# Second layer of a two-layer decoder: the first pair's triangular solution in two parts, and two receptance mixes with priority

## The chip, the cores and the metric

The kernel runs on one core of one Trainium2 chip. A core has a matrix engine (PE, with its weight loads shown apart as PEld), a vector engine (DVE), a scalar engine (ACT), GpSimd (POOL) and a queue engine (SP) that only issues transfers; each works through its own instructions in order, and they meet through semaphores. The metric is the device time of one execution, in microseconds. A time is given as the median of several runs.

## The reference, cut to what matters

Two residual layers on x of 512 rows by 2048 columns, in float32. Layer 0 is differential attention and is not touched. Layer 1 is RWKV-7 time mixing with 32 heads of 64:

```python
p = h @ w_in
p = p + (token_shift(p) - p) * mu                 # mix of each row with the row before it
r, k, v, g, dw, da = jnp.split(p, RW_SPLITS, axis=-1)
w_log = -softplus(-(w0 + tanh(dw) @ decay_up)) - 0.5
decay = jnp.exp(-jnp.exp(w_log))
a = sigmoid(a0 + da @ iclr_up)
kk = heads(k * k_k); kk = kk / max(norm(kk), 1e-12)
k = k * (1.0 + (a - 1.0) * k_a)
# per row t:  sa = S @ (-kk_t)
#             S  = S * decay_t + sa (kk_t * a_t)^T + v_t k_t^T
#             y_t = S @ r_t
y = group_norm(y) + sum(r * k * r_k) * v
x = x + (y * silu(g)) @ w_out
```

The scan over rows is computed in 8 chunks of 64 rows. Within a chunk the recurrence of `sa` becomes a triangular system, which is solved once per chunk and head, so that the chunks then need only matrix products.

## The kernel before, in words

Every product with a weight matrix is done in three passes (`mm3`, L122): operands are split into a high and a low half, and the three products high·high, low·high, high·low add up in one PSUM bank. Weights arrive by transfer in `wraw`; ACT makes the high half `wh` (L105) and DVE the low half `wl` (L106), 8 blocks of 128 by 128 at a time.

**Rounds.** Layer 1 works on 16 pairs of heads (128 channels), j = 0 to 15, in one loop of `layer1`. A projection of one pair (`proj`, through `unit_chan`) is 48 products in a row. Round j has, in the order of the program:

- from j = 1 on, the start of the scan of pair j-1 (`chain(...).step`), whose later steps are put between the products of the round, a fixed number of products apart (`tick`);
- `stage2(j)`: DVE scales the receptance of pair j into `p.AR` (L1291) and makes the product `rf` from it (L1292);
- the projection of the values, `proj(2, j)`. Behind its 18th product comes `behind`: `gram` (PE products `pt` L1301 and `gp` L1318, which read `p.AR` and `p.BK`), the copies of `gp` to SBUF, their transfer to DRAM (`ltd`, SP), the masks on POOL (L1339, L1341) and `t_solve`;
- `stage_v` (mix of the values L1144/L1145, and `y`, L1448, which reads a bank of tag `pd`), in round 1 the first gate's projection, then `begin(j + 1)` (projection and mix of the keys of the next pair, and its decays), in rounds 3 and later a gate, then `receptances(j + 1)`: the projection and its mix (`shift_mix`, ACT L1144 and then DVE L1145).

**The solution.** `t_solve(j)` loads `LT` back from DRAM in another layout and makes 31 steps on DVE. Step i is two instructions, L1377 (`tmpl<-LT,Tm`) and L1379 (`Tm<-Tm,tmpl`); it works on (31-i) columns by (i//4 + 1) rows, which is how a step is recognised by its size in the trace (step 19 is 12·5 = 60 elements a partition). Each step needs the step before. Then L1386 scales the result and SP writes it to DRAM (`td<-Tm`, L1387). For pairs 3 to 14 the steps come in three parts (`PARTS` = 0, 21, 29, 31), of which the second and third are held until steps of the scan have been issued. For pairs 0, 1, 2 and 15 all 31 steps are issued at once.

**What follows it.** `t_combine` reads `td` back into `TT` by four transfers on SP (L1406), and DVE transposes (L1416) give `T1`. PE then makes the small products `px` (L1422, in the bank of tag `pd`; later L1433), and then the scan of the 8 chunks (`sm`, L1510, L1521, L1528) begins. For pair 0 the transposes come 64 products after the start of round 1 (`leads = {1: 64, ...}`) and `px` 8 products later (`GAP_T`).

**The order.** A planner orders the instructions of each engine. It plays the program through with its own estimates of durations and, each time an engine is free, picks the ready instruction with the lowest number. The number is the place in the program, less the offset of `high_priority`: 2000 for `urgent` functions (`split_w`, `shift_mix`), 3000 (`SCAN`) for steps of a chain, 4000 (`SOLVE`) for the solution, 8000 (2·`SOLVE`) for `p.AR` of pairs 1 and 2. Offsets of nested blocks add up. `issue_after(x)` puts what its block holds behind x on x's engine. On the chip each engine keeps the planned order, whether or not the estimates were right.

## Time and profile before

| what | us |
|---|---|
| median of 3 runs (lowest to highest) | 2072.66 (2071.66 to 2075.58) |
| profiled execution, its own time | 2070.32 |
| span of its instructions | 2068.6 |
| PE busy | 2051.0 |
| PEld busy | 1680.1 |
| DVE busy | 1605.3 |
| ACT busy | 1122.7 |
| POOL busy | 383.2 |

The span runs from the first to the last instruction of the program; the execution's own time has a little around it. Layer 1's rounds begin about 940 us into the span and the rounds 0 to 2, of which the change speaks, lie between 940 and 1130 us. Products on PE overlap: one is shown with 0.39 us, but the next begins 0.23 us after it, so that in the rows it is the starts and the idle times that count.

In a timeline row the first number is the start in us from the start of the span, the second the duration in us, then engine, line, operation, output<-inputs and shapes; a bracket at the end is the time for which the engine sat idle before, and what released it. In a row of the chain of waits the first number is the start and the second what it takes on the chain.

### The profile page before, as it was taken

The page shows a single profiled execution, that of the slowest core. Times are in us where ns is not written, and L with a number is a line of the kernel's source. Part 1 is how long each engine was busy: PE and PEld are TensorE (multiplying, and loading weights), DVE is VectorE, ACT ScalarE, POOL GpSimd, SP SyncE. Part 2 cuts the span into 40 slices and gives each one's busy share as a digit, 9 for nine tenths or more (in the row PEclk, how much of TensorE's full clock was granted, in tenths as well). Part 3 has the DMA queues.
Part 4 walks back from the last instruction along what each step waited for, and adds up shares of the span by engine and source line. Part 5 has one row for each costly group of instructions (what it writes and reads, how often), then busy time and mean ns, then how long its engine had stood idle before and what let it go on. Part 6 is the DMA issues. An engine that isn't in the chain of part 4 may idle for free.

```text
span 2068.6 us, 34162 instructions
## 1 busy us (share of the span) xinstructions
PE 2051.0 (99%) x11948; PEld 1680.1 (81%) x11948; DVE 1605.3 (78%) x4113; ACT 1122.7 (54%) x2238; POOL 383.2 (19%) x765
## 2 busy tenths in 40 slices
PE   9999999999999999999999999999999999999999
PEld 7888888888888888878777778888888888877887
DVE  6988988888888976475778887877777878777645
ACT  5765656555666544355555555555555555545322
POOL 1021211102011100101122322222222222232001
PEclk9999999999999999999999999999999999999999
DMA  8487978778787965723323223233333232346565
GB/s 273 140 177 195 172 177 183 166 195 162 189 179 169 263 223 174 170 86 108 102 82 98 86 85 97 79 104 98 97 97 97 86 96 81 112 127 203 184 164 121
DMA packets 158653, 294.61 MB, mean 142 GB/s; under 512 B 64416, under 2 KB 81824, under 8 KB 158480
## 3 DMA queue, kind: packets, MB, share of 16 engines
q1 hardware_dynamic: 110912, 184.91, 28.6%
q0 software_dynamic: 24928, 87.21, 22.4%
q10 hardware_dynamic: 22640, 20.30, 3.0%
q8 instruction: 94, 1.54, 0.3%
q14 instruction: 79, 0.65, 0.1%
HBM read 268.71 MB, written 23.66 MB: 141 GB/s over the span
## 4 chain that ended last, share of the span: by engine, by line
PE 86%; DVE 9%; ACT 2%; DMA 1%; issue 1%; ACTq 0%; SPq 0%; DVEq 0%; POOLq 0%
PE pp L122 43%; PE pp L573 22%; PE pt L122 5%; DVE wl L106 2%; PE sm L1510 2%; PE gp L1318 1%; PE sc L122 1%; PE o L122 1%; PE sm L1528 1%; PE sm L1521 1%; PE lora L122 1%; PE z L122 1%; DVE tmpl L1377 1%; DMA pair<-in_xT_dram 1%; PE Y L1550 1%
## 5 line engine op out<-in xcount | busy, mean ns | idle before, releaser
L106 DVE TENSOR_TENSOR wl<-wraw,wh 128x1024 fp32r<-128x1024 f32 (+2 forms) x291 | 356.6, 1225 | 189.6 <-ACT wh L105 179.3
L105 ACT CAST wh<-wraw 128x1024 fp32r<-128x1024 f32 (+2 forms) x291 | 303.6, 1043 | 271.7 <-PE pp L122 135.3
L122 PE MATMUL pp<-hL,wh 128*128 128x512 f32 x1024 | 414.6, 405 | 0.0
L122 PE MATMUL pp<-hH,wl 128*128 128x512 f32 x1024 | 413.5, 404 | 0.0
L122 PE MATMUL pp<-hH,wh 128*128 128x512 f32 x1024 | 413.2, 403 | 0.0
L122 PEld LDWEIGHTS pp<-hH,wh 128*128 128x128 f32 x1024 | 193.3, 189 | 34.5 <-issue 0.4
L122 PEld LDWEIGHTS pp<-hL,wh 128*128 128x128 f32 x1024 | 193.3, 189 | 33.6
L122 PEld LDWEIGHTS pp<-hH,wl 128*128 128x128 f32 x1024 | 193.5, 189 | 32.3
L573 PE MATMUL pp<-wh,hH 128*128 128x512 f32 x448 | 177.0, 395 | 0.0
L573 PE MATMUL pp<-wh,hL 128*128 128x512 f32 x448 | 176.0, 393 | 0.0
L122 PE MATMUL pp<-wh,hH 128*128 128x512 f32 x372 | 146.8, 395 | 1.7 <-ACT hH L1104 1.7
L122 PE MATMUL pp<-wh,hL 128*128 128x512 f32 x372 | 147.0, 395 | 0.1
L122 PE MATMUL pp<-wl,hH 128*128 128x512 f32 x372 | 146.5, 394 | 0.5 <-DVE wl L106 0.5
L1377 DVE SCALAR_TENSOR_TENSOR tmpl<-LT,Tm 128x60 f32<-128x60 f32 (+24 forms) x496 | 134.4, 271 | 13.3
L573 PE MATMUL pp<-wl,hH 128*128 128x512 f32 x448 | 140.4, 392 | 0.0
L1516 POOL COPY SA<-VS 64x64 f32<-64x64 f32 x224 | 56.7, 253 | 416.7 <-DVE VS L1532 381.9
L1379 DVE TENSOR_TENSOR Tm<-Tm,tmpl 128x60 f32<-128x60 f32 (+24 forms) x496 | 104.2, 210 | 11.7
L1513 ACT COPY rhs<-sm 64x64 f32<-64x64 f32 x256 | 52.8, 206 | 91.8 <-PE sm L1510 89.2
L573 PEld LDWEIGHTS pp<-wl,hH 128*128 128x128 f32 x448 | 84.5, 189 | 17.1
L573 PEld LDWEIGHTS pp<-wh,hH 128*128 128x128 f32 x448 | 84.2, 188 | 17.3 <-issue 0.3
L573 PEld LDWEIGHTS pp<-wh,hL 128*128 128x128 f32 x448 | 84.3, 188 | 16.2
L1523 ACT COPY VS<-sm 64x64 f32<-64x64 f32 x256 | 52.7, 206 | 72.6 <-PE sm L1521 66.0
(402 smaller groups left out, 4380.7 us busy)
## 6 DMA issues: line engine op xcount, KB each, us to landing
wraw<-in_rw_w_in_dram SPq DMA_DIRECT2D x128, 512.0 KB
wraw<-in_da_w_in_dram SPq DMA_DIRECT2D x75, 512.0 KB
wraw<-in_da_w_in_dram POOLq DMA_DIRECT2D x28, 512.0 KB, 6.5
wraw<-in_da_w_out_dram SPq DMA_DIRECT2D x26, 512.0 KB
wraw<-in_rw_w_out_dram SPq DMA_DIRECT2D x26, 512.0 KB
Ta<-in_da_w_in_dram POOLq DMA_DIRECT2D x21, 512.0 KB, 5.4
Tb<-in_da_w_in_dram POOLq DMA_DIRECT2D x21, 512.0 KB, 5.4
Tc<-in_da_w_in_dram POOLq DMA_DIRECT2D x21, 512.0 KB, 5.4
```

The source lines that it names most:

```text
L105: a = nc.scalar.copy(hi[:, ks], raw[:, ks])
L106: d = nc.vector.tensor_sub(lo[:, ks], raw[:, ks], hi[:, ks].bitcast(F32))
L122: m = nc.tensor.matmul(out, a, b, start=s, stop=e, skip_group_check=skip)
L573: m = nc.tensor.matmul(out[t][:], x, wt[lo][:, k, :], start=first, stop=end and lo == 1 and k == KG - 1, skip_group_check=True)
L1318: m = nc.tensor.matmul(gp[h][:, i * P : (i + 1) * P], BK[r_, c0 + i, :, :], p.AR[r_, c0 + i, :, :], start=True, stop=True)
L1377: nc.vector.scalar_tensor_tensor(tt, LT[:, i : i + 1, i + 1 :].to_broadcast([P, s, n]), n2[:, i : i + 1], Tm[:, 0:s, i : i + 1].to_broadca ...
L1379: nc.vector.tensor_add(Tm[:, 0:s, i + 1 :], Tm[:, 0:s, i + 1 :], tt)
L1510: nc.tensor.matmul(sm[:, 0:P], both(p.G[:, c, 0]), both(VS[:, c]), start=True, stop=True)
L1513: nc.scalar.copy(rhs[r_, :], sm[r_, h * C : h * C + C])
L1516: nc.gpsimd.tensor_copy(p.SA[r_, c - 1, :], VS[r_, c, h, :])
L1521: nc.tensor.matmul(sm[:, P : P + C], both(g.TT[j % 2][:, c]), rhs[:], start=True, stop=True)
L1523: g.copied = nc.scalar.copy(VS[r_, c, h, :], sm[r_, P : P + C])
```

## The change

Three things are altered, all in layer 1.

1. The solution of pair 0 is made in two parts, steps 0 to 18 and steps 19 to 30. The first is issued where all of it was issued before. The second is issued at the head of round 1, right after `stage2(1)`, with an offset of 4000 (no longer 8000, since it is no longer inside `t_solve`) and, on DVE, behind the instruction that scales the receptance of pair 1 (L1291). The final scaling and the transfer `td<-Tm` go with the second part.
2. In round 1 `stage2` stands before the start of the scan of pair 0, in place of after it.
3. The mixes of the receptances of pairs 1 and 2 get an offset of 8000 on top of the 2000 that `shift_mix` has. Their projections keep theirs.

`t_solve` now takes the list of parts: (0, 19, 31) for pair 0, `PARTS` for pairs 3 to 14 as before, (0, 31) for pairs 1, 2 and 15, which is one part, issued at once as before.

```diff
     with g.tc.high_priority(offset=2 * SOLVE if 0 < j <= LAG else 0):
-        nc.vector.tensor_mul(p.AR[:, :, 1, :], ..., p.E[:, :, 1:])
+        scaled = nc.vector.tensor_mul(p.AR[:, :, 1, :], ..., p.E[:, :, 1:])
...
+    return scaled
...
     def parts():
-        for a, b in zip(PARTS, PARTS[1:]):
-            with g.tc.high_priority(offset=SOLVE), g.tc.issue_after(g.state.ins) if a and split else ExitStack():
+        for a, b in zip(split, split[1:]):
+            with g.tc.high_priority(offset=SOLVE), g.tc.issue_after(g.state.ins) if a else ExitStack():
                 steps(a, b)
...
-            if split:
-                yield
+            yield
...
         def receptances(j):
-            return shift_mix(g, proj(0, j), P, *mus(g, 0, j), "r", 1)
+            ps = proj(0, j)
+            with tc.high_priority(offset=2 * SOLVE if 0 < j <= LAG else 0):
+                return shift_mix(g, ps, P, *mus(g, 0, j), "r", 1)
...
+            if j == 1:
+                g.state = stage2(g, j, r, p)
+                next(pairs[0].solve)
+                g.state = None
             if j:
                 others = ...
                 chain(g, j - 1, pairs[j - 1], 5, *gaps, others, leads.get(j, GAP_D - GAP_T)).step(g)
-            stage2(g, j, r, p)
+            if j != 1:
+                stage2(g, j, r, p)
...
-                loaded = t_solve(g, j, p, LAG < j < D // P - 1)
+                loaded = t_solve(g, j, p, (0, 19, HALF - 1) if j == 0 else PARTS if LAG < j < D // P - 1 else (0, HALF - 1))
```

More of the change, by code (lines that the diff above doesn't have):

```diff
@@ L1290, in stage2 @@
     with g.tc.high_priority(offset=2 * SOLVE if 0 < j <= LAG else 0):
-        nc.vector.tensor_mul(p.AR[:, :, 1, :], r[:].rearrange("p (c t) -> p c t", c=NC_), p.E[:, :, 1:])
+        scaled = nc.vector.tensor_mul(p.AR[:, :, 1, :], r[:].rearrange("p (c t) -> p c t", c=NC_), p.E[:, :, 1:])
     nc.vector.scalar_tensor_tensor(r[:], r[:], col("hrk"), p.f[:], ALU.mult, ALU.mult)
     p.rf = r
+    return scaled
 def gram(g, j, p, before):
```

## The prediction

> **What bounds the kernel now.** First the page's busy times, then the waits of PE in rounds 0 to 4 of layer 1 (930 to 1240 us), then stretches of 20 us.

> ```profile
> span 2068.6 us, 34162 instructions
> PE 2051.0 (99%) x11948; PEld 1680.1 (81%) x11948; DVE 1605.3 (78%) x4113; ACT 1122.7 (54%) x2238; POOL 383.2 (19%) x765
> ```
> ```profile
> PE sm L1510 <- DVE VS L1532: 2.6, 7, 0.9
> PE gp L1318 <- DVE AR L1291: 0.9, 1, 0.9
> PE pt L1459 <- DVE y L1448: 0.2, 1, 0.2
> PE px L1422 <- DVE y L1448: 0.2, 1, 0.2
> ```
> ```profile
> 980.00:1000.00 20.00, 20.00 (x89) 16.49 (x89) 18.70 (x54) 10.44 (x17) 0.00 (x0) 1.00 0.23 80
> 1000.00:1020.00 20.00, 18.94 (x142) 15.16 (x141) 14.22 (x32) 8.09 (x14) 5.44 (x13) 1.00 0.46 128
> 1240.00:1299.00 59.00, 59.00 (x439) 48.91 (x434) 46.72 (x130) 32.72 (x77) 16.27 (x38) 1.00 0.32 94
> ```

> The columns of a stretch are its length, then PE, PEld, DVE, ACT and POOL busy, and the granted clock. PE is busy for all of 980 to 1000 and of 1240 to 1299, at full clock: the later rounds have nothing to give. In the whole span PE is idle for 2068.6 - 2051.0 = 17.6 us, and the change adds or removes no PE instruction. From 1000 to 1020, where the second pair's receptance is scaled and the first pair's solution ends, PE is idle 20.00 - 18.94 = 1.06 us, which is the 0.87 of `gp` and the 0.19 of `px` below. That is about all that the edits of round 1 can win at their own places.

> The trace's LDWEIGHTS says something else at first sight. [...] By it PE has 19% to spare (81% on the page), and what 1000 to 1020 loses against the full stretch before it is 16.49 - 15.16 = 1.33 us in place of 1.06: the ceiling of the gain would be 1.33. The trace bears that out only in part: the full stretch has itself 16.49 of 20.00, 82%, without any idle time, so 81% is near to what this kernel's products allow.

> Now the place itself, in the rows of the engines in order of time.

> ```profile
> 996.90 1.06 ACT L105 CAST wh<-wraw 128x1024 fp32r<-128x1024 f32 x1 [3.10 <-PE pp L122]
> 997.86 0.68 ACT L1144 ACTIVATE mixr<-pp,omu 128x512 f32<-128x512 f32 x1
> ```
> ```profile
> 997.94 0.28 DVE L1377 SCALAR_TENSOR_TENSOR tmpl<-LT,Tm 128x60 f32<-128x60 f32 x1
> 998.25 0.22 DVE L1379 TENSOR_TENSOR Tm<-Tm,tmpl 128x60 f32<-128x60 f32 x1
> ...
> 999.55 1.22 DVE L106 TENSOR_TENSOR wl<-wraw,wh 128x1024 fp32r<-128x1024 f32 x1
> 1000.68 0.27 DVE L1377 SCALAR_TENSOR_TENSOR tmpl<-LT,Tm 128x54 f32<-128x54 f32 x1
> 1000.87 0.74 DVE L1145 SCALAR_TENSOR_TENSOR mixr<-pp,mu,mixr 128x511 f32<-128x511 f32 x1
> 1001.53 0.21 DVE L1379 TENSOR_TENSOR Tm<-Tm,tmpl 128x54 f32<-128x54 f32 x1
> 1001.65 0.69 DVE L1291 TENSOR_TENSOR AR<-mixr,E 128x512 f32<-128x512 f32 x1
> ```
> ```profile
> 1001.10 0.42 PE L1301 MATMUL pt<-k,ones 128*32 128x128 f32 x8
> 1002.40 2.06 PE L1318 MATMUL gp<-AR,BK 64*128 64x128 f32 x32 [0.87 <-DVE AR L1291]
> ...
> 1006.33 0.39 PE L122 MATMUL pp<-hH,wl 128*128 128x512 f32 x1
> ```

> The receptance's mix is ready for DVE when ACT ends its share, at 997.86 + 0.68 = 998.54, but DVE comes to it at 1000.87, after steps 19 to 21 of the solution (the first of them at 997.94) and a `wl`. `AR` follows at 1001.65, and PE, in order, stands 0.87 before `gp`. What comes after on the chain of waits is the solution:

> ```profile
> 1008.95 0.43 DVE Tm L1386
> 1009.43 2.17 DMA td<-Tm
> 1011.69 3.56 DMA TT<-td
> 1015.27 0.44 DVE T L1416
> 1015.71 0.63 DVE mixv L1145
> 1016.37 0.45 DVE T L1416
> 1016.85 0.70 DVE y L1448
> ...
> 1017.59 0.69 PE px L1422 x32
> ```

> So the next thing for which PE stands, 15 us later, hangs on the end of the solution, and with only 0.19 us of idle PE (the `px` row of the waits) the two are all but tied. That is the centre of the forecast.

> **The parts of the change.**

> *Mix with priority, and steps 19 to 30 behind `AR`.* Steps 19, 20, 21 and the first half of 22 no longer stand ahead of `AR`. DVE reaches the end of step 18 at 997.9. With the `wl` first (its ACT half ends at 996.90 + 1.06 = 997.96) it is 998.0 + 1.2 = 999.2, then the mix 0.7 and `AR` 0.7: 1000.6. With the mix first it is 998.54 + 0.7 + 0.7 = 999.9. PE could take `gp` some 0.4 after `pt` starts at 1001.10, so at 1001.5: both orders are early. The wait of 0.87 goes: -0.87, and PE is 0.87 ahead from `gp` on.

> *The end of the solution.* From 997.9 to 1009.4 DVE stands still only for hand-overs, and the same instructions have to be done before the final scaling in both kernels. Moving steps behind `AR` changes their order and not their sum. What is added is the idle time in which DVE has no more step it may do and the mix is not ready: nothing if the `wl` fills it (997.96 against 997.9, so 0.05), and 998.54 - 997.91 = 0.63 if the mix is planned ahead of the `wl`. I take 0.05: on ACT the `wl`'s half is planned ahead of the mix's, so it is the `wl` that is there first. An offset of 4000 in place of 8000 costs nothing, since the weights' 2000 and the scan's 3000 stay behind it. It could end earlier by what is let in between two steps now and later then: at most the `wl`, 1.2.

> *What is late next.* PE now comes to `px` at 1017.59 - 0.19 - 0.87 = 1016.53, and the transposes and `y` (which holds the bank of `px`) are done at 1016.85 + 0.70 + 0.05. So PE stands until 1017.59 + 0.05, 1.11 us in place of 0.19. What `gp` gave, `px` takes: -0.87 + 0.92 = +0.05.

> *`stage2` ahead of the scan's start in round 1.* The scan's start issues four transfers on SP (`TT`) that wait for `td` anyhow, at 1011.69, ten us after `AR`; on DVE and PE it issues nothing before `px`'s transposes. It moves past no work that is ready: 0.

> *The transfers that go with the second part.* One `td<-Tm` (1009.43 on the chain), still followed by `TT`. What stands behind it on SP:

> ```profile
> 1009.92 1.05 SPq L1330 DMA_DIRECT2D ltd<-G  x2
> 1011.02 0.44 SPq L78 DMA_DIRECT2D wraw<-in_rw_w_in_dram  x1
> 1011.69 2.81 SPq L1406 DMA_DIRECT2D TT<-td  x4
> 1014.54 0.45 SPq L1330 DMA_DIRECT2D ltd<-G  x1
> 1015.09 6.03 SPq L78 DMA_DIRECT2D wraw<-in_rw_w_in_dram  x2
> ```

> `gp` comes 0.87 earlier, so its copies and `ltd<-G` do too; they stand behind `td` or `TT` now and lose nothing. 0.

> *Round 2's mix.* The chain of waits shows `pt` and `gp` of round 2 back to back:

> ```profile
> 1063.72 0.36 PE pt L1301 x8
> 1064.07 1.99 PE gp L1318 x32
> ```

> There is no wait to remove; an earlier mix shifts other DVE work by its 0.7 us, and the only DVE work for which PE stands in that stretch is the scan's `VS` (2.6 us over seven places in 300 us). 0, between -0.4 and +0.7.

> The sum is +0.05 us on a profiled execution of 2070.32 with a span of 2068.6. That execution lies 2.34 below the median of the runs, 2072.66, and a difference carries over: 2072.7.

> **Rivals.**

> *The gain is kept.* DVE takes the values' mix and `y` ahead of the two transposes, which stand idle for `TT` until 1015.27. Then the transposes end at 1015.27 + 0.9 = 1016.2, before PE is there (1016.53), and both waits are gone: -1.06, 2071.6. For it: the planner holds the solution's end for later than before, and the values' mix then comes first. Against: nothing on the chip changes by more than tenths.

> *The `wl` starves.* If it is planned behind the whole second part it ends near 1009.4, where the first product that reads it comes at 1006.33 - 0.87 = 1005.46. PE stands 3.9, less the 0.87 and the 0.19: +2.9, 2075.6. Against: before, it slipped in between two steps, and the chain of steps leaves such holes still.

> *Slower: `TT` falls behind a weight load on SP.* The place is SP at 1015.09, where a load stands that goes when its buffer comes free. If the planner holds the solution's end for so late that this load is put ahead of `TT`, the four transfers begin at 1015.5 and not at 1011.69, and `px`, which is tied to them, moves by all of it: +3.8, with the idle 0.63 +4.4, 2077.1. It decides from the moment that the planner's estimate of the end moves by 1015.09 - 1011.69 = 3.4 us. Against: the second part has about four steps more behind `AR` than before (19 to 22), at 0.53 us each (997.94 to 998.47 above), some 2 us.

> *Not what it says.* The wait of `gp` stays, if the DVE reaches `AR` late all the same: 0, 2072.7; the same time as the forecast.

> **How the numbers follow.** The wait moves to `px`: 0.55. Gain kept: 0.25. `wl` late: 0.06. `TT` behind a load: 0.06. No effect: 0.08. A measurement of this kernel can tell about 0.2%, 4.1 us, from no change; of the cases only the `TT` one passes it. Runs of the same kernel spread from 1.0 below to 2.9 above the median, so I give each side a little for that: faster 0.04, same 0.88, slower 0.08. The range reaches from the kept gain in a low run, 2072.66 - 1.06 - 1.0 = 2070.6, to the late `wl`, 2075.6, and by a quarter of the scan's 2.6 us of waits (0.6) further at both ends, since round 1's order on DVE may shift for or against `VS`: 2070.0 to 2076.2.

> **What would show it.** Right: no row of PE `gp` waiting for `AR`; on DVE `AR` at 999.9 to 1000.6 with twelve steps behind it (the first of 60 elements); `td<-Tm` at 1009.4 to 1010.1; PE at `px` waiting about 1.1 for `y` or the transposes; the rounds from 1240 on shifted as a whole by tenths. Kept gain: `mixv` and `y` ahead of both L1416. Wrong: `td<-Tm` after 1011, a wait of a `pp` product for `wl`, or rounds from 1240 on that are not 59 us apart.

## The result, and the profile after

The changed kernel takes 2076.11 us (median of 22 runs, 2072.93 to 2078.64), the kernel before 2070.30 (22 runs, 2069.19 to 2075.58). The ratio is 1.0024, with a 95% interval of 1.0018 to 1.0029: slower by some 5 us (5.8 between the medians), a little more than the 0.2% that the prediction took as the least that can be told. The forecast was 2072.7, with 0.88 on no difference that can be told. The time came out just inside the upper end of its range, 2076.2, and that is luck: the range stood on the 2072.66 of three runs, while 22 runs put the kernel before at 2070.30. The same terms on that base end at 2073.8. How the loss comes about is not what the prediction said. The profiled execution took 2076.41, 6.1 more than the one of before (2070.32).

First the page's busy times, then the two largest waits of PE in 930 to 1240 us (total, times, longest), both of the changed kernel:

```profile
span 2074.7 us, 34161 instructions
PE 2053.3 (99%) x11948; PEld 1680.3 (81%) x11948; DVE 1606.4 (77%) x4113; ACT 1124.2 (54%) x2238; POOL 381.4 (18%) x765
```
```profile
PE px L1422 <- DVE T L1416: 3.9, 2, 3.2
PE sm L1510 <- DVE VS L1532: 2.0, 5, 0.9
```

The row of `gp` is gone, as the change intends. In its place stands `px`, with 3.9 us where it had 0.2. Matmuls are as many as before; PE's busy time grew by 2.3 us all the same; some 1.7 of it is the clock (3.41 us at half, below).

PE's order is the same in both kernels, so the same product can be looked up in both traces. How far the changed kernel is behind at some of them:

| product | before | after | behind | added since the row above |
|---|---|---|---|---|
| `pt`, ahead of all that changed | 975.48 | 976.18 | 0.70 | 0.70 |
| `gp` of round 1 | 1002.40 | 1002.15 | -0.25 | -0.95 |
| `px` of round 1, its third | 1017.64 | 1021.37 | 3.73 | 3.98 |
| sixth product behind `px` | 1019.48 | 1024.65 | 5.17 | 1.44 |
| `sm` of the seventh chunk of the first pair's scan | 1050.63 | 1055.20 | 4.57 | -0.60 |
| `gp` of round 6 | 1296.75 | 1303.21 | 6.46 | 1.89 |
| end of the span | 2068.6 | 2074.7 | 6.1 | -0.4 |

The first 0.70 is a difference between two executions. In round 6 PE stood 1.6 for `AR`; the run split_only below, whose planned order is the same, shows no such wait, so it too belongs to the execution. What is left is round 1: -0.95 + 3.98 + 1.44 = 4.5 us.

Round 1 on DVE, in order of time (start, duration, instruction):

```profile
998.36 0.23 DVE L1380 TENSOR_TENSOR Tm<-Tm,tmpl 128x65 f32<-128x65 f32 x1
998.68 1.23 DVE L106 TENSOR_TENSOR wl<-wraw,wh 128x1024 fp32r<-128x1024 f32 x1
999.83 0.74 DVE L1145 SCALAR_TENSOR_TENSOR mixr<-pp,mu,mixr 128x511 f32<-128x511 f32 x1
1000.60 0.69 DVE L1291 TENSOR_TENSOR AR<-mixr,E 128x512 f32<-128x512 f32 x1
1001.21 0.28 DVE L1378 SCALAR_TENSOR_TENSOR tmpl<-LT,Tm 128x60 f32<-128x60 f32 x1
...
1009.56 0.23 DVE L1378 SCALAR_TENSOR_TENSOR tmpl<-LT,Tm 128x8 f32<-128x8 f32 x1
1009.71 1.22 DVE L106 TENSOR_TENSOR wl<-wraw,wh 128x1024 fp32r<-128x1024 f32 x1
1010.85 0.17 DVE L1380 TENSOR_TENSOR Tm<-Tm,tmpl 128x8 f32<-128x8 f32 x1
1011.05 0.42 DVE L1387 TENSOR_TENSOR Tm<-Tm,LT 128x256 f32<-128x256 f32 x1
...
1013.35 0.74 DVE L1145 SCALAR_TENSOR_TENSOR mixv<-pp,mu,mixv 128x511 f32<-128x511 f32 x1
1014.20 0.69 DVE L1448 TENSOR_TENSOR y<-pt,mixv 128x512 f32<-128x512 f32 x1
1019.88 0.44 DVE L1416 STREAM_TRANSPOSE T<-TT 64x256 f32<-64x256 f32 x1 [4.99 <-DMA TT<-td]
```

`AR` follows step 18, one `wl` and the mix, and twelve steps follow it. But a second `wl` (1009.71) has slipped between the two halves of the last step. From the end of step 18 (998.59) to the end of the scaling (1011.47) it is 12.88 us; before, it was 1009.37 - 997.91 = 11.46. So the solution is 1.42 late, 1.22 of it that `wl`. After it DVE has `mixv` and `y` done by 1014.9, and then stands 4.99 us for a transfer.

The queues tell why. SP (changed kernel), then POOL's load of the second pair's `LT`, changed kernel and kernel before:

```profile
1004.93 1.81 SPq L1331 DMA_DIRECT2D ltd<-G  x4
1010.96 0.35 SPq L78 DMA_DIRECT2D wraw<-in_rw_w_in_dram  x1
1011.54 0.39 SPq L1388 DMA_DIRECT2D td<-Tm  x1
1018.01 1.81 SPq L1406 DMA_DIRECT2D TT<-td  x4
```
```profile
1011.77 2.00 POOL L1365 DMA_DIRECT2D LT<-ltd  x4 [4.53 <-DVE Tm L1387]
```
```profile
1016.97 2.00 POOL L1364 DMA_DIRECT2D LT<-ltd  x4 [4.31 <-DMA ltd<-G]
```

Before, only one of the second pair's four `ltd<-G` stood ahead of `td<-Tm` on SP, two and a weight load behind it, and the fourth behind `TT` (1014.54). POOL's `LT` loads, which need all four and the buffer that the end of the solution gives free, could not start before 1016.97. Now all four `ltd<-G` and the weight load of 1010.96 are planned ahead of `td`. The weight load is issued 0.6 us before `td`. The last thing for which the `LT` loads wait is now the solution itself (the releaser in the row is `Tm`, no longer `ltd`), so they start 0.2 us behind `td`. The solution's transfers run beside both. The chain of waits of the changed kernel:

```profile
1011.05 0.44 DVE Tm L1387
...
1011.54 6.34 DMA td<-Tm
...
1018.88 1.97 DMA TT<-td
1020.88 0.45 DVE T L1416
...
1021.37 1.05 PE px L1422 x30
```

`td` took 6.34 in place of 2.17 us. The 1.97 of `TT` is not to be set against the 3.56 of before: it runs from the third of the four transfers, the 3.56 from the first (on SP the four begin at 1018.01). From the end of the scaling to the start of the last transpose it is 1020.88 - 1011.47 = 9.4 us in place of 1016.37 - 1009.37 = 7.0.

What PE does in that time, changed kernel, and the stretches (length; PE, PEld, DVE, ACT, POOL busy; granted clock; DMA share; GB/s):

```profile
1016.81 0.39 PE L122 MATMUL pp<-hH,wl 128*128 128x512 f32 x1
1020.37 0.24 PE L1422 MATMUL px<-T,G 32*32 32x32 f32 x2 [3.17 <-DVE T L1416]
1021.37 1.05 PE L1422 MATMUL px<-T,G 32*32 32x32 f32 x30 [0.76 <-DVE T L1416]
...
1022.95 0.63 PE L122 MATMUL pp<-hL,wh 128*128 128x512 f32 x1
1023.37 0.63 PE L122 MATMUL pp<-hH,wl 128*128 128x512 f32 x1
```
```profile
1012.00:1017.00 5.00, 5.00 (x23) 3.94 (x21) 2.58 (x3) 1.49 (x3) 1.72 (x4) 1.00 0.90 231
1017.00:1021.40 4.40, 0.47 (x5) 0.16 (x5) 0.93 (x3) 1.04 (x1) 2.55 (x7) 1.00 0.32 57
...
1022.50:1024.90 2.40, 2.40 (x6) 1.92 (x7) 2.00 (x10) 1.96 (x4) 0.00 (x0) 0.51 0.60 212
1024.90:1030.00 5.10, 5.10 (x54) 4.05 (x54) 3.54 (x15) 1.14 (x4) 0.00 (x0) 1.00 0.04 17
```

The transfer engines are 90% busy while `td` is under way (54% in the kernel before, from 1009.4 to 1011.6). PE stands 3.17 + 0.76 = 3.93 us, and when it goes on its granted clock is 0.51: products that start 0.23 apart at full clock start 0.43 apart. That is the 1.44 of the table.

### The profile page after: what moved, and what is told of

It reads as the page before. It is cut to its first block, busy times and chain, and to the rows that moved or that the text cites. A ratio compares the mean times of both kernels' runs of the same rounds, so it can differ in the third digit from the quotient of the medians.

```text
span 2074.7 us, 34161 instructions
## 1 busy us (share of the span) xinstructions
PE 2053.3 (99%) x11948; PEld 1680.3 (81%) x11948; DVE 1606.4 (77%) x4113; ACT 1124.2 (54%) x2238; POOL 381.4 (18%) x765
## 4 chain that ended last, share of the span: by engine, by line
PE 88%; DVE 7%; DMA 2%; ACT 2%; issue 1%; ACTq 0%; SPq 0%; POOL 0%; DVEq 0%; POOLq 0%
PE pp L122 43%; PE pp L573 24%; PE pt L122 5%; DVE wl L106 2%; PE sm L1510 1%; PE gp L1319 1%; PE sc L122 1%; PE o L122 1%; PE sm L1528 1%; PE sm L1521 1%; PE lora L122 1%; PE z L122 1%; DVE tmpl L1378 1%; PE Y L1550 1%; PE pt L296 1%
## 5 line engine op out<-in xcount | busy, mean ns | idle before, releaser
L106 DVE TENSOR_TENSOR wl<-wraw,wh 128x1024 fp32r<-128x1024 f32 (+2 forms) x291 | 356.1, 1224 | 189.2 <-ACT wh L105 184.0
L105 ACT CAST wh<-wraw 128x1024 fp32r<-128x1024 f32 (+2 forms) x291 | 303.7, 1044 | 273.6 <-PE pp L122 141.7
L122 PE MATMUL pp<-hL,wh 128*128 128x512 f32 x1024 | 414.7, 405 | 0.0
L122 PE MATMUL pp<-hH,wh 128*128 128x512 f32 x1024 | 413.3, 404 | 0.0
L122 PE MATMUL pp<-hH,wl 128*128 128x512 f32 x1024 | 413.3, 404 | 0.0
L122 PEld LDWEIGHTS pp<-hH,wh 128*128 128x128 f32 x1024 | 193.4, 189 | 34.8 <-issue 0.4
L122 PEld LDWEIGHTS pp<-hL,wh 128*128 128x128 f32 x1024 | 193.4, 189 | 33.7
L122 PEld LDWEIGHTS pp<-hH,wl 128*128 128x128 f32 x1024 | 193.6, 189 | 32.5
L122 PE MATMUL pp<-wh,hH 128*128 128x512 f32 x372 | 146.5, 394 | 1.9 <-ACT hH L1104 1.9
L122 PE MATMUL pp<-wl,hH 128*128 128x512 f32 x372 | 146.8, 395 | 0.7 <-DVE wl L106 0.5
L122 PE MATMUL pp<-wh,hL 128*128 128x512 f32 x372 | 146.9, 395 | 0.1
```

The lines of the kernel that those rows point to most:

```text
L105: a = nc.scalar.copy(hi[:, ks], raw[:, ks])
L106: d = nc.vector.tensor_sub(lo[:, ks], raw[:, ks], hi[:, ks].bitcast(F32))
L122: m = nc.tensor.matmul(out, a, b, start=s, stop=e, skip_group_check=skip)
```

## The experiments

Each is timed against the kernel before on the same chip (medians 2071.07, 2071.50, 2071.25 and 2071.35; the times in the expectations go by 2070.3, so about 1 us lower). The theory: the split lets the solution end later in the plan, what the planner then puts ahead of its transfers slows these, and the priority of the mixes does nothing. The rivals: the priority does it; the late `wl` alone does it; the order on SP's queue does it, and not what shares the transfer engines.

### Which part of the change: mix_only and split_only

mix_only is the kernel before with the priority alone:

```diff
-            return shift_mix(g, proj(0, j), P, *mus(g, 0, j), "r", 1)
+            ps = proj(0, j)
+            with tc.high_priority(offset=2 * SOLVE if 0 < j <= LAG else 0):
+                return shift_mix(g, ps, P, *mus(g, 0, j), "r", 1)
```

> The kernel before with only the priority of the two receptance mixes; the solution of pair 0 stays in one piece. Theory T (transfers: the loss is the wait of px for the transposes, because td<-Tm takes 6.3 us in place of 2.2 beside a weight load and the load of LT): nothing of that is touched, so td<-Tm stays at 2.2 and the time within 1 us of the kernel before, 2069.4 to 2071.3. Theory R (rival: the loss comes from the priority of the mixes, which reorders DVE in rounds 1 and 2): the whole loss, +5 us, is here.

Measured: 2071.45, ratio 1.0004 (0.9995 to 1.0012). `gp` still waits 0.7, `px` 0.5; `td` takes 2.17, `TT` 3.71.

split_only is the changed kernel without the priority:

```diff
-            ps = proj(0, j)
-            with tc.high_priority(offset=2 * SOLVE if 0 < j <= LAG else 0):
-                return shift_mix(g, ps, P, *mus(g, 0, j), "r", 1)
+            return shift_mix(g, proj(0, j), P, *mus(g, 0, j), "r", 1)
```

> The changed kernel without the priority of the two receptance mixes. Its planned order is the changed kernel's on every engine, so the priority has nothing left to do once part two stands behind AR: +5 us against the kernel before, 2075 to 2076, td<-Tm near 6 us, px waiting 3 to 4, the clock at half for some microseconds. A theory in which the priority matters beside the split expects another time. It also shows again how far one kernel's executions differ in these places.

Measured: 2075.92, ratio 1.0024 (1.0014 to 1.0035), the whole loss. Its planned order is that of the changed kernel on every engine, so it is a second execution of the same program:

```profile
1010.46 5.55 DMA td<-Tm
```

The priority is inert; the split, with `stage2` moved ahead of the scan's start, makes the loss. Whether it is the splitting itself or the lower offset of its second part (4000 in place of 8000) that lets the second `wl` in was not run.

### What the `LT` loads do: lt_early

In the kernel before, nothing of the split, the second pair's four `ltd<-G` get a higher priority, so that they stand ahead of `td` on SP:

```diff
-    with g.tc.high_priority(offset=SOLVE if j == D // P - 1 else 0):
+    with g.tc.high_priority(offset=3 * SOLVE if j == 1 else SOLVE if j == D // P - 1 else 0):
```

> The kernel before, with one change: the four transfers ltd<-G of pair 1 go out on SP ahead of td<-Tm, so that POOL can load LT of pair 1 as soon as the solution of pair 0 has ended, together with td<-Tm. Theory T with LT as a cause: td<-Tm takes 4 to 6 us in place of 2.2, px waits 2 to 4 us, and the time is 2072 to 2075. If the weight load ahead of td<-Tm is the only cause (it stays behind td<-Tm here): no change, within 0.5 us. Theory S (only the late end of the solution counts): no change. Theory R: no change.

Measured: 2077.56, ratio 1.0032 (1.0020 to 1.0044). The chain of waits:

```profile
1009.20 2.16 DMA td<-Tm
...
1011.43 8.00 DMA TT<-td
```

The solution is not late here, and the weight load stands 1.1 us behind `td`. POOL's `LT` loads start at 1010.21, `TT` takes 8.00 us in place of 3.56, and PE stands 4.2 at `px`. One priority, with no split, makes the same loss and more: the early `LT` loads are enough. The expectation was missed in two ways: it looked for the delay in `td` and not in `TT`, and its 2072 to 2075 were too little.

### Taking the suspects away one by one: lt_behind, load_behind, both_behind

All three are the changed kernel. lt_behind puts the last of the four `ltd<-G` behind `TT`, which holds the `LT` loads until 1021.9:

```diff
+                with g.tc.issue_after(g.blocks) if j == 1 and half and h else ExitStack():
                     nc.sync.dma_start(
                         out=g.ltd[j % 2, half, h, :, 0:HALF].rearrange("c s t -> s c t"),
```

> The changed kernel, with the last ltd<-G of pair 1 put behind the four transfers TT<-td on SP, so that LT of pair 1 is loaded later, as it was before. The weight load still goes ahead of td<-Tm, and the solution ends as late as in the changed kernel. Theory T with LT as the main cause: td<-Tm back to 2.5 to 4 us, the wait of px from 3.9 to about 1 to 2, 2071.5 to 2073. With the weight load as the main cause: td<-Tm stays near 5 to 6 and the time near 2075. Theory R: no change against the changed kernel, 2075.

Measured: 2074.89, ratio 1.0018 (1.0009 to 1.0026).

```profile
1010.26 5.21 DMA td<-Tm
...
1016.42 1.89 DMA TT<-td
```

With no `LT` load near, and the weight load 0.6 us ahead, `td` still takes 5.21: of the 6.34 of the changed kernel, the weight load makes most. PE stands 1.9 + 0.7 at `px`, and the clock stays full; this execution, 2072.65, is 2.2 below the median of its eleven.

load_behind puts the weight load behind `td`:

```diff
+    late = c == KT + 2 and k0 == 8
+    with g.tc.issue_after(g.last) if g.last and not queue else ExitStack(), \
+            g.tc.issue_after(g.wrote) if late else ExitStack():
```

> The changed kernel, with the weight load that went out on SP 0.6 us ahead of td<-Tm put behind it. LT of pair 1 is still loaded at the same time, and the solution ends as late. Theory T with the weight load as the main cause: td<-Tm back to 2.5 to 3.5 us, the wait of px from 3.9 to about 1, 2071 to 2072.5. With LT as the main cause: td<-Tm 4 to 5 us, about 2074. Theory R: no change, 2075.

Measured: 2074.89, ratio 1.0019 (1.0010 to 1.0028). With the weight load 0.5 us behind it and the `LT` loads 0.2, `td` takes 3.64; `TT` takes 3.35, PE stands 2.5 + 0.2. `td` lies between the two cases of the expectation, the time at that of the `LT` loads. This execution, 2073.09, is the fastest of its eleven.

> The changed kernel, with both the weight load and the load of LT of pair 1 kept out of the way of td<-Tm (the weight load behind td<-Tm on SP, the last ltd<-G behind the four TT<-td). The solution still ends 1.2 us late, behind the wl between the halves of its last step. Theory T (the two loads make the transfers slow, and this is all of the loss but the late end): td<-Tm 2.2 and TT<-td 3.6 to 4, px waits 1.5 to 2, the clock stays at full, gp does not wait: 2071 to 2072. If the late end of the solution (theory S) were the larger part: 2073 or more.

Both edits: 2075.18, ratio 1.0014 (1.0005 to 1.0023). The 2071 to 2072 of the theory was missed; the time falls under the expectation's other case, the late end. In the profile `td` took 3.44, `TT` 2.48 and PE stood 1.4 + 0.2; but that execution, 2070.57, is the fastest of its eleven, 4.6 below their median. So the profile does not show what most executions of this kernel lose. Taking both suspects away while the `wl` stays late does not bring the time back.

### With the solution in time again: wl_lt_behind and wl_behind

Both are the changed kernel with that late `wl` put behind the solution's last scaling; the plan of the weight load then falls behind `td` by itself:

```diff
-            d = nc.vector.tensor_sub(lo[:, ks], raw[:, ks], hi[:, ks].bitcast(F32))
+            with g.tc.issue_after(g.solved0) if parts and parts[1] == 3 * KT and k0 == 0 else ExitStack():
+                d = nc.vector.tensor_sub(lo[:, ks], raw[:, ks], hi[:, ks].bitcast(F32))
...
+                    g.solved0 = g.solved if j == 0 else g.solved0
```

wl_lt_behind has the edit of lt_behind as well.

> The changed kernel, with the wl of the first gate's projection held behind the last scaling of the solution of pair 0 on DVE, and the last ltd<-G behind TT<-td on SP. With the wl goes the weight load that needs its buffer: it falls behind td<-Tm by itself. Theory T and S together: the solution ends 1.2 us sooner than in the changed kernel, td<-Tm 2.2, TT<-td 3.6, px waits 0.5 to 1.2 and gp does not: 2069.8 to 2071, as the kernel before or a little under it, which is the sum of the prediction. If something else of the split costs time, 2072 or more.

Measured: 2072.84, ratio 1.0007 (0.9998 to 1.0016): the loss is gone within the uncertainty, which leaves room for 3 us. The expected 2069.8 to 2071 was missed: PE stands 2.7 us at `px` and not 0.5 to 1.2, and the clock falls behind it. wl_behind is the same without the edit of lt_behind, so that the `LT` loads go early:

> The changed kernel with the `wl` of the third gate's first tile put behind the last scaling of the first pair's solution on DVE, and nothing else: on SP the weight load falls behind `td<-Tm` by itself, while all four `ltd<-G` of the second pair stay ahead of it. If the 1.2 us of the `wl` (with the weight load that follows from it) is what matters, `td<-Tm` leaves at about 1009.5 and the time is that of wl_lt_behind, 2072 to 2073.5 (ratio 1.000 to 1.001). If POOL's loads of `LT` beside `td` and `TT` matter by themselves, as in lt_early, `TT<-td` takes 6 us or more, PE stands some 3 us at `px`, and the time is 2075 to 2077 (ratio 1.002 to 1.003).

Measured: 2077.76, ratio 1.0029 (1.0020 to 1.0038). The chain of waits and POOL's `LT` loads, first wl_lt_behind, then wl_behind:

```profile
1009.07 2.16 DMA td<-Tm
...
1011.30 4.79 DMA TT<-td
```
```profile
1017.40 2.00 POOL L1367 DMA_DIRECT2D LT<-ltd  x4 [5.11 <-DMA ltd<-G]
```
```profile
1010.52 2.16 DMA td<-Tm
...
1012.75 7.25 DMA TT<-td
```
```profile
1010.74 2.00 POOL L1366 DMA_DIRECT2D LT<-ltd  x4 [3.52 <-DVE Tm L1388]
```

The two edits differ in one transfer's place; ahead of `px` the order differs besides only on POOL and in which of `y` and the second transpose comes first. (They ran on two chips, each against its own kernel before.) With the `LT` loads at 1017.40 `TT` takes 4.79 us and PE stands 2.7; with the loads at 1010.74 `TT` takes 7.25, PE stands 4.8, and the median is 4.9 us higher. The rival "the late `wl` alone" falls with this. But the late `wl` counts too: both_behind and wl_lt_behind, on one chip, differ in its place and what follows from it (the weight load goes out 0.44 and 1.09 us behind `td`), and their medians differ by 2.3 us. lt_behind, which has the `LT` loads late and the `wl` and the weight load as the split leaves them, loses 3.8 us. So the early `LT` loads are enough for most of the loss, the late `wl` with its weight load is too, and the two do not add up.

### Is it the queue, or the engines behind it? td_act

The changed kernel with the first pair's `td<-Tm` issued on ACT's queue, where nothing stands ahead of it:

```diff
-                    nc.sync.dma_start(out=g.td[j % 2].rearrange("q l t -> l q t"), in_=Tm[:])
+                    (nc.sync if j else nc.scalar).dma_start(out=g.td[j % 2].rearrange("q l t -> l q t"), in_=Tm[:])
```

> The changed kernel with the one transfer td<-Tm of pair 0 issued on ACT in place of SP, so that it stands in another queue than the weight load that goes out ahead of it. If td<-Tm is slow because it stands behind the weight load in the same queue: 2.5 to 4 us, px waits 1 to 2, 2072 to 2073.5. If it is slow because the transfer engines are shared by all queues (the weight load and the load of LT from POOL together): 5 to 6 us still, 2075.

Measured: 2075.05, ratio 1.0018 (1.0009 to 1.0027).

```profile
1011.58 5.95 DMA td<-Tm
```

5.95 in place of 6.34: in a queue of its own `td` is nearly as slow. A queue that it has to itself does not help here; what is left as the cost is what is under way at the same time: the weight load, which goes out on SP 0.5 us ahead of it, at 1011.04, and POOL's `LT` loads 0.3 behind it, at 1011.84. From 1012 to 1017 the transfer engines of this run are 94% busy, at 237 GB/s. How they divide their time between the queues no run shows.

### Could PE be kept from standing? px_later and px_filled

px_later is the changed kernel with the transposes and `px` of round 1 moved 20 products back:

```diff
-                leads = {1: 64, LAG: 18, LAG + 1: 42}
+                leads = {1: 84, LAG: 18, LAG + 1: 42}
```

> The changed kernel with the transposes and px 20 products later in round 1 (a lead of 84 in place of 64): PE has 4.5 us of other products where it stood. Loads, td<-Tm and the end of the solution stay as in the changed kernel. If the loss is PE standing for px (3.9 us) and the clock after it (1.4 us): both go, and the time is 2069.5 to 2071.5, unless the scan of pair 0, 4.5 us later from there, runs into the end of round 1. If the loss came from the slow transfers in another way (the solution of pair 1, or weights that come late): 2074 or more.

Measured: 2077.67, ratio 1.0027 (1.0017 to 1.0038). The expected 2069.5 to 2071.5 was missed. Round 1's wait at `px` is gone. Three of the five rows of PE's waits in 930 to 1240:

```profile
PE sm L1521 <- ACT rhs L1513: 2.0, 3, 1.3
PE px L1422 <- DVE T L1416: 2.0, 1, 2.0
PE sm L1510 <- DVE VS L1535: 0.8, 1, 0.8
```

A scan that starts later gives the time back piece by piece: 2.0 at `rhs`, 0.8 at `VS`, and 2.0 at `px` of round 4. In all PE stands 7.5 us in that stretch, and 6.5 in the changed kernel.

px_filled is the changed kernel with 14 products put ahead of `px` of round 1. They are written into the bank of `px` and thrown away, so it does work that nobody needs:

```diff
+    if j == 0:
+        for _ in range(14):
+            nc.tensor.matmul(px[:], g.hH[0][:, 0:P], g.hH[0][:], start=True, stop=True)
```

> The changed kernel with 14 products more on PE right ahead of px in round 1, whose result is thrown away (px writes over it): 14 x 0.227 = 3.2 us of PE work where PE stands for 3.2 to 3.9 us. If the half clock after the wait is a consequence of PE standing: the wait falls to below 1 us, the granted clock stays at 1.00 and the products behind px keep 0.23 us apart; where the changed kernel's execution has lost 1.4 us to the clock the time is lower by that, 2073.5 to 2074.5; where an execution has a short wait, the added products cost up to 3 us. If the half clock has another cause (the size or kind of the px products): it is there still, and the time is 2075 to 2076.

Measured: 2078.01, ratio 1.0032 (1.0022 to 1.0043). The first of PE's rows is the filling, which now stands where the idle time was:

```profile
1015.58 3.33 PE L1420 MATMUL px<-hH 128*128 128x512 f32 x14
```

From 1018 to 1024 the granted clock is 1.00. But a new wait of 1.9 us follows (`sm` for `VS`, from 1028.98), and behind it, from 1030.98 on, the clock is at half for 3.41 us. So the loss of clock goes with the standing still wherever that falls, and the time is not better. The expected 2073.5 to 2074.5 was missed. Neither run mends the late chain; both only move its cost.

## Why the prediction's mechanism was wrong, step by step

The time fell inside the range by the high base alone (above); no term of the sum and no rival had what happened.

- **The wait of `gp` goes: right.** `AR` at 1000.60, with the `wl` first, as the step said; `gp` at 1002.15, ahead of before's by 0.95 in the table (0.87 foreseen).
- **"The end of the solution", +0.05: wrong.** It is +1.42. The step counted what DVE must do before the scaling and took for granted that the same `wl` blocks would lie ahead of it; it even allowed one fewer. One more slipped in.
- **"What is late next": the right place, a wrong size.** `px` takes the wait, as the step said, but 3.93 us of it and not 1.11, because the step moved the transfers along unchanged (`td` 2.17, measured 6.34).
- **"The transfers that go with the second part", 0: this is the step that failed most.** It read the order of SP from the trace of before ("`ltd<-G` ... stand behind `td` or `TT` now and lose nothing") and kept it. The planner made another: all four `ltd<-G` and a weight load ahead of `td`. That the `LT` loads wait for the four `ltd` and for the end of the solution, and so start with `td` as soon as the four are early, could be read in the code and was not. The two transfers and the `wl` together put the last transpose at 1020.88 in place of 1016.37, 4.5 us; the rounds of that execution were 0.7 late anyhow.
- **The rival "`TT` falls behind a weight load on SP", 0.06: near in kind and price, wrong in its place.** A load was planned ahead, and its +3.8 to +4.4 is near the measured 5 to 5.8. But it stands ahead of `td`, not of `TT`; it was the load that stood 1.6 us behind `td` (1011.02 - 1009.43) and not that of 1015.09, so that less lateness was enough than the 3.4 that the rival asked for (on the chip it is 1.42); and POOL's loads were not in it.
- **The rival "the gain is kept", 0.25: half of it came.** `mixv` and `y` do run ahead of both transposes (1013.35, 1014.20). It brings nothing, for the transposes wait for `TT` until 1019.88.
- **Round 2's mix and the priority, 0: right** (mix_only, split_only).
- **Weight-load share.** PEld's 81% is 81% again in a kernel 6 us longer. It could not have shown the loss, nor did it show a reserve.
- **Not in any step: the clock.** 1.44 us of the profiled execution, and more on average (below).

What stays open: the medians differ by 5.8 us and round 1 of the profiled execution explains 4.5. Part of the rest is the clock. Each execution's mean granted clock is on record, to three digits; one less that, times the span, is 4.2 us on average for the changed kernel's 22 executions, and 0.8 to 1.4 for those of the kernel before on the four chips of the experiments. By this estimate up to some 3 us of the loss come by the clock. It also differs between executions: both_behind's profiled one has 1.000 and its median one 0.999, which is some 2 of the 4.6 us between them; the rest of these 4.6 is not explained. More than the 1.06 us that PE stood in round 1 was never to be won there, and the best variant, wl_lt_behind, is no faster than the kernel before.

## What to carry to other kernels

Before a chain's end is moved, list what that end sets free: here a buffer, and with it four loads that then compete with the very transfer for which the next stage waits. An order read from the trace of before holds only as long as the planner sees the same end; ask of each transfer queued near it how little lateness puts it on the other side. And price a standing PE above its length: here a stall of 1.9 us was enough to cost the clock as well (3.41 us at half, after others 6.83), and filling or shifting the stall did not bring back the chain behind it.

## What the hardware showed that was not expected

**A transfer's time depends on what starts beside it.** `td<-Tm`, the same 128 by 256 floats each time, took 2.16 to 2.17 us when the nearest weight load was issued 1.1 us or more behind it (also in wl_behind, where the `LT` loads came 0.2 behind), 3.44 and 3.64 with a weight load 0.4 to 0.5 behind, and 5.2 to 6.3 with a weight load 0.5 to 0.6 ahead. `TT<-td`, straight behind a fast `td`, took 3.6 to 4.8 without the `LT` loads, and 7.25 and 8.00 with them under way.

```profile
1027.57:1030.98 3.41, 1.51 (x9) 0.98 (x8) 3.07 (x13) 1.31 (x3) 0.41 (x2) 1.00 0.00 0
1030.98:1034.39 3.41, 3.41 (x11) 2.63 (x12) 3.34 (x8) 1.35 (x5) 0.50 (x2) 0.50 0.07 12
```
```profile
1015.56:1018.97 3.41, 1.88 (x9) 1.22 (x7) 0.09 (x1) 0.00 (x0) 2.54 (x7) 1.00 0.80 221
1018.97:1022.38 3.41, 2.20 (x38) 1.81 (x39) 2.13 (x4) 2.39 (x5) 0.00 (x0) 1.00 0.35 130
```
```profile
1015.93:1019.34 3.41, 0.44 (x3) 0.13 (x2) 0.78 (x2) 1.04 (x1) 2.56 (x7) 1.00 0.37 62
1019.34:1022.75 3.41, 3.25 (x35) 2.74 (x36) 3.01 (x10) 1.96 (x4) 0.00 (x0) 0.50 0.63 210
1022.75:1026.16 3.41, 3.41 (x39) 2.37 (x37) 2.98 (x13) 0.00 (x1) 0.00 (x0) 0.50 0.20 80
```

In layer 1 of all thirteen traces a step at full clock in which PE stood 1.90 us or more is followed by one at half clock, and one in which it stood 1.57 or less is not (the 1.90 is px_filled's step from 1027.57, the 1.57 the changed kernel's from 1301.31). After a step at half clock the clock stays at half if PE stood in it at all (0.15, 0.18 and 1.10 us in split_only, lt_early and wl_behind) and is full again if it did not. (In the first 25 us of the span the border is less sharp: 1.69 us cost the clock in td_act, 1.74 did not in lt_behind.) So the length of a stall does not settle its price, but where it falls does: the 2.51 us of load_behind lie across two steps, 1.53 and 0.98, and keep the clock; the 1.90 of px_filled lie in one and lose it. The steps do not follow the program: half clock begins at 1021.42 in the changed kernel and at 1019.35 in split_only, whose order is the same. Nor need PE stand for a whole step to lose the clock: 1.90 us of 3.41 were enough in px_filled.
